# A decoder trunk on one core: a 64-byte smaller filler in front of the feed-forward's tiles, and the first weight load cut in two

## The chip, the core and the metric

The kernel runs on one core of a Trainium2 chip. The core has a matrix engine (TensorE; PE in the profile, with the loads of its stationary operand shown apart as PEld), VectorE (DVE), ScalarE (ACT), GpSimd (POOL) and SyncE (SP), and 16 DMA engines that move data between device memory and the on-chip memory SBUF. SBUF has 128 partitions; an address below is a byte offset within a partition. The metric is device time in microseconds of one execution; lower is better.

## The reference

Two layers, 256 tokens of width 1024, float32. Each layer is a sandwich: half a SwiGLU feed-forward, a token mixer, half a SwiGLU feed-forward. Layer 0 mixes with a sparse attention (compressed blocks, selected blocks, window), layer 1 with a sliding window with sinks. A final norm follows.

```python
def swiglu(x, w_gu, w_down):
    g, u = jnp.split(x @ w_gu, 2, axis=-1)
    return (jax.nn.silu(g) * u) @ w_down
...
for i in range(DEPTH):          # DEPTH = 2, D_MODEL = 1024, D_FF = 2816, SEQ = 256
    x = x + 0.5 * swiglu(rmsnorm(x, ffn1_norm[i]), ffn1_w_gu[i], ffn1_w_down[i])
    h = rmsnorm(x, mix_norm[i])
    y = nsa_mixer(h, ...) if kind == 0 else swa_mixer(h, ...)
    x = x + y
    x = x + 0.5 * swiglu(rmsnorm(x, ffn2_norm[i]), ffn2_w_gu[i], ffn2_w_down[i])
return rmsnorm(x, final_norm)
```

There are so four feed-forwards, called ffn 0 to ffn 3 here, in the order ffn 0, sparse attention, ffn 1, ffn 2, window attention, ffn 3.

## The kernel before, in words

**Precision.** Every float32 operand of a product is split into a rounded part `hi` (type float32r) and a rest `lo = value - hi`, and a product is the sum of three: hi by hi, hi by lo, lo by hi. Weights are split on the way: a piece of 1024 columns is loaded (`raw`, 5 buffers), ACT writes `hi`, DVE or POOL writes `lo` (4 buffers each). In the profile these are the lines L169 (load), L153 or L155 (`hi`), L183 (`lo`).

**A feed-forward.** The first half makes, for each of 22 blocks of 128 hidden units, the gate and the up part (`gu`). There the weights are the stationary operand (128 by 128) and the normalized, transposed input `xh` is the moving one: for each of 8 parts of the width, one matmul of 512 columns (`hi` of the weight by `hi` and `lo` of the input side by side) and one of 256 columns (`lo` of the weight by `hi` of the input), for gate and up each, in turn 512, 256, 512, 256. The result leaves through ACT and DVE, is gated, and is split into `hh` and `hl` (128 by 256 each), which stay in SBUF: 22 tiles of each, in the feed-forward's own pool. The second half (`dn`) turns the roles round: for each of the 22 blocks and each of the two halves of the tokens, a 128 by 128 part of `hh` or `hl` is the stationary operand and the split weight (`dn_h`, `dn_l`) moves, 512 columns wide: 22 x 2 x 3 = 132 matmuls for a block of 512 output columns, 264 in all. In ffn 3 the output columns are cut 512, 256, 256 (`LASTW`), so it has 132 matmuls of 512 columns and 264 of 256.

**Where tiles lie.** Pools take SBUF one after the other in the order in which they are opened: `const`, `weights`, `acts`, `small`, and then, one at a time in the same room, those of the feed-forwards, the two attentions, and `last`, which is opened before ffn 3 and stays in front of it. A tile called `fill_...` is never read or written; it only moves what comes behind it. Offsets inside tiles do the same on purpose: the `hi` part of the feed-forward's first weights starts 192 bytes into its tile (`PLACE_GU`), the inputs of the two attentions 64 bytes into theirs (`PLACE_NORM`), and ffn 3 has 448 bytes of filler of its own (`PLACE_H`). The table gives the places in the built program, as a remainder by 256.

| operand | stationary in | start, remainder by 256 |
|---|---|---|
| `gu_h` (hi of gate and up weights) | `gu` | 192 |
| `gu_l` (lo of the same) | `gu` | 0 |
| `hh`, `hl` of ffn 0, 1, 2 | `dn` | 64 |
| `hh`, `hl` of ffn 3 | `dn` | 0 |
| `xh` of the attentions | projections in (`nin`, `sin`) | 64 |
| `qs`, `vv` of the attentions | scores, weighted sums | 64 |
| `dn_h`, `dn_l`, `xh` of the feed-forwards | moving | 0 |

**The start.** The first norm and the first gate and up block are written by hand in order (`Norm.first`). TensorE multiplies zeros, then turns the first half of x, then takes the parts of the width as their weights come, in the order of `FIRST_K`. The first 2048 columns of weights come as four loads of 512. The first piece is split by two engines: POOL makes `hi` and `lo` of its columns 0 to 255, ACT and DVE those of 256 to 511 (L317). SP issues loads in order; the tile layer counts the completion of loads on eight counters in turn, and a load waits until the load eight before it has landed.

Of the kernel before, what the change touches and what calls it, by code (L numbers as in the profile page):

```python
# [91 lines left out]
def trunk_kernel(tc, x_in, wgu, wdn, nsa_in, nsa_w1, nsa_out, swa_in, swa_out, small, fgain, consts, out):  # L92
    nc = tc.nc
    from contextlib import ExitStack, contextmanager

    with ExitStack() as es:
# [3 lines left out]
        sp = es.enter_context(tc.tile_pool(name="small", bufs=1))  # L100
        pp = es.enter_context(tc.tile_pool(name="psum", bufs=1, space=PSUM))

        def fill(pool, name, n):

            pool.tile([P, n // 4], F32, name=f"fill_{name}")
# [7 lines left out]
        nc.gpsimd.memset(mhalf, -0.5)  # L113
        warm = cp.tile([P, NT], F32, name="warm")
        fill(cp, "const", 672)
        fill(sp, "small", 320)

        def mm(o, w, m, start, stop):
            nc.tensor.matmul(o, w, m, start=start, stop=stop)  # L119
# [7 lines left out]
        def s_bank(name):  # L127
            return pp.tile([P, 512], F32, tag="sc", bufs=BANKS["sc"], name=name)
# [31 lines left out]
        class Weights:  # L160
# [3 lines left out]
                self.src, self.name, self.kind, self.parts = src, name, name.rstrip("0123"), {}  # L164
                self.place = place

            def fetch(self, o, w, queue=nc.sync):
                raw = wp.tile([P, PIECE], F32, tag="raw", bufs=BUFS["raw"], name=f"{self.name}_r{o}")
                self.last = queue.dma_start(raw[:, :w], self.src[:, o:o + w]).ins  # L169
                return raw  # L170

            def split(self, o, raw, w, engines=None, starts=(0,)):
# [30 lines left out]
        def transposed(kp, norm, th, tl, tb, engine=None):  # L203

            ps = s_bank(f"xt{norm}_{kp}")
            for kk in range(2):
                for t in range(NT):
                    c = ((2 * kp + kk) % 4) * P
                    nc.tensor.transpose(ps[:, kk * S + t * P:kk * S + (t + 1) * P], x[t][kp // 2][:, c:c + P], ident)  # L209
            both = split_tile(f"xh{norm}_{kp}", PLACE_NORM[norm])  # L210
            hi, lo = both[:, :, 0, :], both[:, :, 1, :]

            def evict(kk):
                k = 2 * kp + kk
                g = prm[:, D_GAIN + norm * KD + k:D_GAIN + norm * KD + k + 1]
                if (engine or pick("xh")) == "A":
                    nc.scalar.activation(hi[:, kk, :], ps[:, kk * S:(kk + 1) * S], AF.Copy, scale=g)
                else:
                    nc.vector.tensor_scalar(hi[:, kk, :], ps[:, kk * S:(kk + 1) * S], g, None, ALU.mult)
                nc.vector.scalar_tensor_tensor(lo[:, kk, :], ps[:, kk * S:(kk + 1) * S], g, hi[:, kk, :],  # L220
                                               ALU.mult, ALU.subtract)
                th[k], tl[k], tb[k] = hi[:, kk, :], lo[:, kk, :], both[:, kk, :, :].rearrange("p a t -> p (a t)")

            return evict
# [4 lines left out]
        def squares(c0, c1, engine="A"):  # L229

            ss = sp.tile([P, NT], F32, tag="ss", bufs=3, name="ss")
            for t in range(NT):
                xc = columns(t, c0, c1)
                junk = ap_.tile([P, 512], F32, tag="junk", bufs=1, name="junk")
                if engine == "V":
                    nc.vector.tensor_tensor_reduce(out=junk[:, :c1 - c0], in0=xc, in1=xc, scale=1.0, scalar=0.0,
                                                   op0=ALU.mult, op1=ALU.add, accum_out=ss[:, t:t + 1])
                else:
                    nc.scalar.activation(junk[:, :c1 - c0], xc, AF.Square, accum_out=ss[:, t:t + 1])
            return ss  # L240

        def mean(j, v, ss):

            if j == 0:
                nc.vector.tensor_scalar(v, ss, 1.0 / D, EPS, ALU.mult, ALU.add)
            else:
                nc.vector.scalar_tensor_tensor(v, ss, 1.0 / D, v, ALU.mult, ALU.add)

        def row_scale(v, name):

            y = sp.tile([P, NT], F32, tag="rs_y", bufs=2, name=f"{name}_y")
            w = sp.tile([P, NT], F32, tag="rs_w", bufs=2, name=f"{name}_w")
            r = sp.tile([P, NT], F32, tag="rs_r", bufs=2, name=f"{name}_r")
            nc.gpsimd.tensor_tensor(y, v, mhalf, ALU.pow)
            nc.vector.tensor_mul(w, y, y)
            nc.vector.scalar_tensor_tensor(w, w, -0.5, v, ALU.mult, ALU.mult)
            nc.vector.scalar_tensor_tensor(r, w, 1.5, y, ALU.add, ALU.mult)
            return r

        class Norm:  # L260
# [18 lines left out]
            def first(self, wts, product, turn_scales):  # L279


                def load_x(t, h, queue):
                    queue.dma_start(x[t][h], x_in[t * P:(t + 1) * P, h * 512:(h + 1) * 512])

                evict = {}

                def turn(*kps):
                    for kp in kps:
                        evict[kp] = transposed(kp, 0, self.h, self.l, self.both, "A")

                def leave(*ks):
                    for k in ks:
                        evict[k // 2](k % 2)

                zeros = ap_.tile([P, 512], BF16, name="zeros")
                nc.vector.memset(zeros, 0.0)
                ps = s_bank("idle")

                def multiply_zeros(n):
                    for _ in range(n):  # L300
                        mm(ps, zeros[:, :P], zeros, True, True)

                multiply_zeros(8)
                load_x(0, 0, nc.sync)
                load_x(1, 0, nc.scalar)
                nc.sync.dma_start(ident, consts[:, C_ID:C_ID + P])
                nc.scalar.dma_start(prm[:, :D_SINK], small[:, :D_SINK])
                raw = [wts.fetch(o, 512) for o in (0, 512)]
                load_x(1, 1, nc.scalar)
                load_x(0, 1, nc.sync)  # L310
                raw += [wts.fetch(o, 512) for o in (1024, 1536)]
                nc.scalar.activation(warm, mhalf, AF.Exp)
                left = squares(0, 512, "V")
                turn(0, 1)
                multiply_zeros(3)
                leave(0, 2)
                wts.split(0, raw[0], 512, ("GG", "AV"), (0, 256))  # L317
                leave(1, 3)
                product(0, 0, 2)
                wts.split(512, raw[1], 512, "AV")  # L320
                turn(2, 3)
                product(0, 1, 3)
                leave(4, 6)
                wts.split(1024, raw[2], 512, "AV")
                leave(5, 7)
                wts.split(1536, raw[3], 512, "AG")
                product(0, 4, 5, 6, 7)
                wts.load(CHUNK, CHUNK, engines="VV")
                right = squares(512, 1024)
                mean(0, self.v, left)  # L330
                mean(1, self.v, right)
                self.r = row_scale(self.v, "n0")
                product(1, *range(KD))
                turn_scales()
# [225 lines left out]
        def weigh(pr, v_of, acc, pool, first, last, name):  # L560

            n_kt = pr.shape[2] // P
            for kt in range(n_kt):
                ps = s_bank(f"{name}_t{kt}")
                for hh in range(4):
                    nc.tensor.transpose(ps[:, hh * P:(hh + 1) * P], pr[:, hh, kt * P:(kt + 1) * P], ident)
                ph = pool.tile([P, 512], F32R, tag="ph", bufs=BUFS["ph"], name=f"{name}_h{kt}")
                pl = pool.tile([P, 512], F32R, tag="pl", bufs=BUFS["pl"], name=f"{name}_l{kt}")
                copy("ph", ph, ps)
                nc.vector.tensor_sub(pl, ps, ph)  # L570
                mm(acc, v_of(kt), ph, first and kt == 0, False)
                mm(acc, v_of(kt), pl, False, last and kt == n_kt - 1)
# [24 lines left out]
        def nsa(norm, nxt):  # L597
            with tc.tile_pool(name="nsa", bufs=1) as mp:
# [213 lines left out]
                def compressed(g, t, acc, first):  # L812
                    nm = f"cm{g}{t}"
                    ce = coarse.pop((g, t))
                    ps = s_bank(f"{nm}_c")
                    for hh in range(4):
                        nc.tensor.transpose(ps[:2 * NCP, hh * P:(hh + 1) * P],
                                            ce[:, hh, :, :].rearrange("p a n -> p (a n)").bitcast(F32), ident)
                    ph = mp.tile([P, 512], F32R, tag="ph", bufs=BUFS["ph"], name=f"{nm}_ch")
                    copy("pc", ph[:2 * NCP], ps[:2 * NCP])  # L820
                    mm(acc, vcs[:2 * NCP, g, :], ph[:2 * NCP], first, True)
# [228 lines left out]
```

## Time and profile before

| | |
|---|---|
| median of 3 runs | 1007.56 us (1004.36 to 1009.14) |
| the profiled execution | 1001.6 us |
| its span, first to last instruction | 999.8 us |
| mean granted TensorE clock | 0.996 of full |
| PE / PEld / DVE / ACT / POOL busy | 97 / 84 / 69 / 56 / 40 % of the span |
| read from device memory | 167.02 MB, 168 GB/s over the span |

PE busy means that some matmul was in flight; matmuls overlap, so how fast they follow each other is read from their starts, not from the busy share. The profiled execution was shorter than the three runs, so differences are taken within it.

### The profile page before, as it was taken

To read this page: it belongs to the slowest core of one execution; us is meant where nothing else is said; L and a number is where in the kernel's file an instruction comes from. 1 tells how busy PE (TensorE), PEld (TensorE's weight loads), DVE (VectorE), ACT (ScalarE), POOL (GpSimd) and SP (SyncE) were. 2 spreads that over 40 slices of the span, in tenths; PEclk is the share of its full clock that TensorE was granted. 3 is DMA by queue.
4 is the path that set the end of the run, shared out by engine and by line. 5 is a ranking of instruction groups with operands and counts; after the bars stand their busy time and mean duration, and the time that the engine had idled before them with its cause. 6 is when DMAs were issued, how large, how long until landed. Compare 5 with 4: busy or idle time off the path is not lost. (4 is left out here: it accounts for less than half of the span.)

```text
span 999.8 us, 15557 instructions
## 1 busy us (share of the span) xinstructions
PE 968.4 (97%) x5626; PEld 836.0 (84%) x5626; DVE 694.2 (69%) x1299; ACT 558.5 (56%) x1042; POOL 401.9 (40%) x400
## 2 busy tenths in 40 slices
PE   8999999998899999999999999999998899999997
PEld 6888888887787788888888888888897688888896
DVE  6887743467898888787435877864279988778533
ACT  6555544356767755555444555544358755655442
POOL 2534353465534225334431334363662013433443
PEclk9999999999999999999999999999999999999999
DMA  8676665543422256665666666656652266666651
GB/s 272 214 217 195 197 189 173 176 148 90 133 74 85 65 184 198 192 196 179 200 183 186 191 191 193 199 172 197 185 151 83 61 204 198 193 195 196 189 178 43
DMA packets 47741, 169.08 MB, mean 169 GB/s; under 512 B 5424, under 2 KB 5680, under 8 KB 47664
## 3 DMA queue, kind: packets, MB, share of 16 engines
q1 hardware_dynamic: 46800, 166.49, 54.8%
q10 hardware_dynamic: 864, 1.60, 0.4%
q8 instruction: 44, 0.72, 0.3%
q14 instruction: 33, 0.27, 0.1%
HBM read 167.02 MB, written 1.05 MB: 168 GB/s over the span
## 5 line engine op out<-in xcount | busy, mean ns | idle before, releaser
L119 PE MATMUL gu<-xh,gu_h 128*128 128x512 f32 x1408 | 479.8, 390 | 1.5 <-POOL gu_h L155 1.5
L119 PE MATMUL gu<-xh,gu_l 128*128 128x256 f32 x1408 | 388.1, 277 | 0.3 <-POOL gu_l L183 0.3
L119 PEld LDWEIGHTS gu<-xh,gu_h 128*128 128x128 f32 x1408 | 263.6, 188 | 55.7 <-POOL gu_h L155 2.0
L119 PEld LDWEIGHTS gu<-xh,gu_l 128*128 128x128 f32 x1408 | 264.1, 188 | 2.3 <-POOL gu_l L183 1.2
L183 DVE TENSOR_TENSOR gu_l<-gu_r,gu_h 128x1024 fp32r<-128x1024 f32 (+1 forms) x177 | 229.1, 1295 | 52.4 <-ACT gu_h L153 51.7
L153 ACT CAST gu_h<-gu_r 128x1024 fp32r<-128x1024 f32 (+2 forms) x178 | 184.6, 1039 | 71.4 <-PE gu L119 53.9
L153 ACT CAST dn_h<-dn_r 128x1024 fp32r<-128x1024 f32 (+1 forms) x89 | 92.5, 1041 | 114.5 <-PE dn L119 104.7
L119 PE MATMUL dn<-dn_l,hh 128*128 128x512 f32 (+1 forms) x396 | 146.7, 370 | 0.0
L119 PE MATMUL dn<-dn_h,hl 128*128 128x512 f32 (+1 forms) x396 | 146.6, 370 | 0.0
L119 PE MATMUL dn<-dn_h,hh 128*128 128x512 f32 (+1 forms) x396 | 146.4, 370 | 0.0
L183 DVE TENSOR_TENSOR dn_l<-dn_r,dn_h 128x1024 fp32r<-128x1024 f32 (+1 forms) x56 | 72.2, 1291 | 105.4 <-ACT dn_h L153 105.3
L158 POOL TENSOR_TENSOR hl<-u,hh 128x256 fp32r<-128x256 f32 x66 | 96.8, 1467 | 103.0 <-DVE hh L155 51.0
L183 POOL TENSOR_TENSOR dn_l<-dn_r,dn_h 128x512 fp32r<-128x512 f32 x66 | 86.8, 1336 | 110.3 <-ACT dn_h L153 109.2
L158 POOL TENSOR_TENSOR ga<-g,rb 128x256 f32<-128x256 f32 x88 | 74.6, 848 | 84.2 <-DVE g L464 79.7
L153 ACT COPY g<-gu 128x256 f32<-128x256 f32 x88 | 32.8, 372 | 109.9 <-PE gu L119 109.8
L119 PEld LDWEIGHTS dn<-dn_h,hh 128*128 128x128 f32 x396 | 74.8, 189 | 13.7
L119 PEld LDWEIGHTS dn<-dn_l,hh 128*128 128x128 f32 x396 | 74.8, 189 | 13.4
L119 PEld LDWEIGHTS dn<-dn_h,hl 128*128 128x128 f32 x396 | 74.8, 189 | 13.4
L119 PE MATMUL nin<-nin_h,xh 128*128 128x256 f32 (+1 forms) x320 | 62.0, 287 | 2.0 <-DVE r_b L489 1.7
L155 POOL CAST hh<-u 128x256 fp32r<-128x256 f32 x44 | 21.5, 488 | 94.1 <-DVE u L158 94.1
L464 DVE TENSOR_TENSOR g<-gu,g 128x256 f32<-128x256 f32 x88 | 37.2, 422 | 29.4 <-ACT g L153 29.0
L442 ACT ACTIVATE th<-ga 128x256 f32<-128x256 f32 x88 | 36.9, 419 | 33.6 <-POOL ga L158 27.6
(243 smaller groups left out, 1361.6 us busy)
## 6 DMA issues: line engine op xcount, KB each, us to landing
gu_r<-in_wgu_dram SPq DMA_DIRECT2D x174, 512.0 KB, 4.4
dn_r<-in_wdn_dram SPq DMA_DIRECT2D x87, 512.0 KB, 4.1
nin_r<-in_nsa_in_dram SPq DMA_DIRECT2D x18, 512.0 KB, 3.6
sin_r<-in_swa_in_dram SPq DMA_DIRECT2D x10, 512.0 KB, 3.5
nout_r<-in_nsa_out_dram SPq DMA_DIRECT2D x8, 512.0 KB, 3.6
sout_r<-in_swa_out_dram SPq DMA_DIRECT2D x8, 512.0 KB, 3.7
cmp_r<-in_nsa_w_dram SPq DMA_DIRECT2D x4, 512.0 KB, 4.4
gu_r<-in_wgu_dram SPq DMA_DIRECT2D x4, 256.0 KB, 5.7
```

What stands on the lines that cost most here:

```text
L119: nc.tensor.matmul(o, w, m, start=start, stop=stop)
L153: nc.scalar.copy(o, i)
L155: (nc.vector if c == "V" else nc.gpsimd).tensor_copy(o, i)
L158: (nc.vector if pick(key) == "V" else nc.gpsimd).tensor_tensor(o, a, b, op)
L183: eng.tensor_tensor(lo[:, q:e], raw[:, q:e], hi[:, q:e], ALU.subtract)
L442: nc.scalar.activation(th, ga, AF.Tanh, scale=0.5)
L464: nc.vector.tensor_tensor(g0, acc[0][:, :S], g0, ALU.add)
```

## The change

The filler in front of the pool `small` is 256 bytes long instead of 320. Everything that lies behind it, the small tiles and all tiles of the feed-forwards and attentions, moves down by 64 bytes; constants, x, weights, inputs `xh` and the attentions' outputs stay. `hh` and `hl` of ffn 0, 1 and 2 then start at remainder 0 by 256, those of ffn 3 at 192, and the attentions' `qs`, `kk` and `vv` at 0.

The first load of 512 columns of weights becomes two loads of 256 columns into the same tile; `fetch` takes a list of widths for that, and is always issued by SP.

```diff
-        fill(sp, "small", 320)
+        fill(sp, "small", 256)
...
-            def fetch(self, o, w, queue=nc.sync):
+            def fetch(self, o, *ws):
+
                 raw = wp.tile([P, PIECE], F32, tag="raw", bufs=BUFS["raw"], name=f"{self.name}_r{o}")
-                self.last = queue.dma_start(raw[:, :w], self.src[:, o:o + w]).ins
+                c = 0
+                for w in ws:
+                    self.last = nc.sync.dma_start(raw[:, c:c + w], self.src[:, o + c:o + c + w]).ins
+                    c += w
                 return raw
...
-                raw = [wts.fetch(o, 512) for o in (0, 512)]
+                raw = [wts.fetch(0, 256, 256), wts.fetch(512, 512)]
```

No instruction of PE, ACT, DVE or POOL is added, removed or moved. On SP one load is added at the start, and from there on the eight completion counters (`DMAHW0` to `DMAHW7`) are one place further for every load. Before, SP's first loads and what they wait for; `x_71` and `x_72` are the two halves of the first 128 tokens, `gu_r` the weights:

```order
L283 DMA x_71<-in_x_dram 128x512
L306 DMA ident<-in_consts_dram 128x128
L169 DMA gu_r_110<-in_wgu_dram 128x512
L169 DMA gu_r_112<-in_wgu_dram 128x512
L283 DMA x_72<-in_x_dram 128x512
L169 DMA gu_r_116<-in_wgu_dram 128x512 [waits DMAHW0_49]
L169 DMA gu_r_118<-in_wgu_dram 128x512 [waits DMAHW1_49]
L169 DMA gu_r_219<-in_wgu_dram 128x1024 [waits DMAHW2_49]
```

And now:

```order
L287 DMA x_71<-in_x_dram 128x512
L310 DMA ident<-in_consts_dram 128x128
L172 DMA gu_r_110<-in_wgu_dram 128x256 x2
L172 DMA gu_r_113<-in_wgu_dram 128x512
L287 DMA x_72<-in_x_dram 128x512 [waits DMAHW0_49]
L172 DMA gu_r_117<-in_wgu_dram 128x512 [waits DMAHW1_49]
L172 DMA gu_r_119<-in_wgu_dram 128x512 [waits DMAHW2_49]
L172 DMA gu_r_220<-in_wgu_dram 128x1024 [waits DMAHW3_49]
```

The wait for the first load, which stood before the third weight load, now stands before `x_72`. On ACT the same place of the program, the split of the first weights between the evictions of the turned x (`xh`), before:

```order
L217 ACTIVATE xh_0_131<-xt_0_126,prm 128x256 [waits DMAHW2_49,PE_49]
L217 ACTIVATE xh_1_137<-xt_1_132,prm 128x256 [waits PE_49]
L153 CAST gu_h_145<-gu_r_110 128x256 [waits DMAHW5_49]
L217 ACTIVATE xh_0_131<-xt_0_126,prm 128x256 [waits DVE_49]
L217 ACTIVATE xh_1_137<-xt_1_132,prm 128x256 [waits DVE_49]
L153 CAST gu_h_163<-gu_r_112 128x512 [waits DMAHW6_49]
```

And now:

```order
L221 ACTIVATE xh_0_132<-xt_0_127,prm 128x256 [waits DMAHW2_49,PE_49]
L221 ACTIVATE xh_1_138<-xt_1_133,prm 128x256 [waits PE_49]
L153 CAST gu_h_146<-gu_r_110 128x256 [waits DMAHW6_49]
L221 ACTIVATE xh_0_132<-xt_0_127,prm 128x256 [waits DVE_49]
L221 ACTIVATE xh_1_138<-xt_1_133,prm 128x256 [waits DVE_49]
L153 CAST gu_h_164<-gu_r_113 128x512 [waits DMAHW7_49]
```

ACT's half of the first weights now waits for a load of its own (counter 6), while POOL's cast of the other half (not shown) still waits for counter 5, on which now only the first 256 columns count.

## Rows read from the trace of the kernel before

**Rows 1.** The page, part 1: busy time and share of each engine.

```profile
PE 968.4 (97%) x5626; PEld 836.0 (84%) x5626; DVE 694.2 (69%) x1299; ACT 558.5 (56%) x1042; POOL 401.9 (40%) x400
```

**Rows 2.** Windows by stage: length, busy by engine (PE first), PEclk, DMA share, GB/s.

```profile
0.00:8.10 8.10, 5.40 (x20) 2.25 (x20) 2.65 (x8) 2.89 (x6) 0.70 (x6) 1.00 0.75 246
...
130.60:193.00 62.40, 62.40 (x274) 50.27 (x273) 22.75 (x28) 26.00 (x32) 25.17 (x20) 1.00 0.60 181
193.00:356.70 163.70, 149.46 (x1012) 129.61 (x1012) 133.87 (x378) 110.49 (x279) 75.28 (x73) 0.99 0.35 107
...
723.60:809.60 86.00, 79.23 (x530) 68.29 (x528) 72.22 (x185) 60.00 (x151) 25.52 (x37) 1.00 0.40 121
809.60:930.60 121.00, 121.00 (x715) 107.07 (x714) 96.84 (x154) 69.77 (x118) 44.74 (x48) 1.00 0.64 191
930.60:992.10 61.50, 61.50 (x397) 56.33 (x396) 26.55 (x31) 23.38 (x32) 28.64 (x24) 1.00 0.42 130
```

**Rows 3.** Groups on PE, 662 to 722 us: shapes, count | busy, mean ns | idle.

```profile
L119 PE MATMUL dn<-dn_h,hh 128*128 128x512 f32 x85 | 33.6, 396 | 0.0
```

**Rows 4.** Groups on PE, 931 to 960 us.

```profile
L119 PE MATMUL dn<-dn_h,hh 128*128 128x512 f32 x44 | 17.1, 389 | 0.0
```

**Rows 5.** Timeline of PE (start, us), first and last of 32 matmuls.

```profile
149.70 0.39 PE L119 MATMUL dn<-dn_l,hh 128*128 128x512 f32 x1
...
156.93 0.40 PE L119 MATMUL dn<-dn_h,hl 128*128 128x512 f32 x1
```

**Rows 6.** The same in ffn 3, first and last of 33 matmuls.

```profile
939.74 0.39 PE L119 MATMUL dn<-dn_l,hh 128*128 128x512 f32 x1
...
946.99 0.39 PE L119 MATMUL dn<-dn_h,hh 128*128 128x512 f32 x1
```

**Rows 7.** The same, ffn 3's narrow blocks, first and last of 60 matmuls.

```profile
969.83 0.28 PE L119 MATMUL dn<-dn_h,hl 128*128 128x256 f32 x1
...
976.90 0.28 PE L119 MATMUL dn<-dn_l,hh 128*128 128x256 f32 x1
```

**Rows 8.** The same, ffn 3's first half, first and last of 43 matmuls.

```profile
849.73 0.39 PE L119 MATMUL gu<-xh,gu_h 128*128 128x512 f32 x1
...
856.87 0.39 PE L119 MATMUL gu<-xh,gu_h 128*128 128x512 f32 x1
```

**Rows 9.** Chain that ended last: start, length, what.

```profile
726.79 9.32 PE sin L119 x80
```

**Rows 10.** Timeline at the start, all engines.

```profile
7.64 0.40 POOL L155 CAST gu_h<-gu_r 128x256 fp32r<-128x256 f32 x1 [6.81 <-DMA gu_r<-in_wgu_dram]
...
8.09 0.73 PE L119 MATMUL gu<-xh,gu_h 128*128 128x512 f32 x2 [1.51 <-POOL gu_h L155]
8.12 0.95 POOL L183 TENSOR_TENSOR gu_l<-gu_r,gu_h 128x256 fp32r<-128x256 f32 x1
```

**Rows 11.** Timeline at the start: SP's issues, and PE's second turn of x.

```profile
1.64 0.90 SPq L169 DMA_DIRECT2D gu_r<-in_wgu_dram  x2
...
2.59 0.43 SPq L283 DMA_DIRECT2D x<-in_x_dram  x1
...
4.30 13.11 SPq L169 DMA_DIRECT2D gu_r<-in_wgu_dram  x9
...
10.06 0.90 PEld L209 LDWEIGHTS xt<-ident,x 128*128 128x128 f32 x8
```

**Rows 12.** Groups on DVE, 541 to 661 us (ffn 2).

```profile
L464 DVE TENSOR_TENSOR g<-gu,g 128x256 f32<-128x256 f32 x21 | 8.9, 423 | 6.8 <-ACT g L153 6.7
```

**Rows 13.** Groups on DVE, 810 to 930 us (ffn 3).

```profile
L464 DVE TENSOR_TENSOR g<-gu,g 128x256 f32<-128x256 f32 x21 | 8.9, 423 | 7.3 <-ACT g L153 7.2
```

**Rows 14.** Waits of PE, 193 to 356.7 us: total, times, longest.

```profile
PE r_q L504 <- POOL r_sq L158: 3.2, 2, 2.1
PE hid L119 <- DVE na_mx L546: 1.9, 1, 1.9
```

**Rows 15.** Windows around a fall of the clock.

```profile
237.00:240.50 3.50, 3.50 (x19) 3.50 (x19) 3.02 (x13) 3.00 (x13) 0.53 (x1) 0.51 0.54 150
```

## The prediction

> **What bounds the kernel now.** I read the page's busy shares first: TensorE has work in flight for 97% of the span [rows 1]. Then the windows by stage [rows 2]: in the second halves of the feed-forwards (130.6 to 193.0 us, 930.6 to 992.1 us) and in the first halves (809.6 to 930.6 us) it is busy for the whole of its window, while no other engine is busy more than four fifths of it and the loads take 0.42 to 0.64 of the DMA engines. So there the time is the number of matmuls times the distance from one start to the next; what shortens that distance shortens the kernel. In the two attentions PE is free for 163.70 - 149.46 = 14.2 us and 86.00 - 79.23 = 6.8 us; there it waits for others. Before 8.1 us it waits for data.
>
> A busy PE hides what matters, so next I read starts. In the second half of ffn 0, 32 matmuls of 512 columns start between 149.70 and 156.93 us: 7.23 / 31 = 233.2 ns each [rows 5]. In the first block of ffn 3, same shape, same moving weights, same split work beside it, 33 start between 939.74 and 946.99: 7.25 / 32 = 226.6 ns [rows 6]. The groups say the same in another way: mean 396 ns in ffn 2, 389 ns in ffn 3 [rows 3, 4]. What is different in the program is where the stationary operands `hh` and `hl` lie: remainder 64 by 256 in ffn 0 to 2, remainder 0 in ffn 3. Neither stretch has a wait. I take it that the load of the next stationary operand, which runs beside the present matmul, disturbs the moving stream by an amount that depends on how the two addresses stand to each other.
>
> **The 64 bytes, ffn 0 to 2.** `hh` and `hl` move to remainder 0, the place of ffn 3 now; the moving weights stay. 3 x 264 = 792 matmuls by 233.2 - 226.6 = 6.6 ns are 5.2 us; by the group means (7 ns) 5.5 us. I take 5.4 us. All of it is on the path: PE is busy throughout, and the split work that feeds it (26.0 us ACT, 22.8 us DVE, 25.2 us POOL in 62.4 us [rows 2]) already keeps up at 226.6 ns in ffn 3. Late next would be the loads, at 181 GB/s now and 186 GB/s then, which the first halves exceed (191).
>
> [...]
>
> **The 64 bytes, ffn 3.** Its `hh` and `hl` leave remainder 0 for 192. For its 264 matmuls of 256 columns, 119.8 ns now (7.07 us / 59 [rows 7]), the nearest row is the first half: there a 256-column matmul runs beside the load of `gu_h`, at 192. A pair takes 7.14 us / 21 = 340.0 ns [rows 8]; less 226.6 for the 512-column one beside `gu_l`, at 0, leaves 113.4. The other row is the window attention's projection, 256 columns beside operands at 64: 9.32 us / 80 = 116.5 ns [rows 9]. I take 113.4: 264 x 6.4 ns = 1.7 us gained. The steps seen are about 6.6 ns; one step the wrong way (126.4) would lose 1.7 us. For its 132 matmuls of 512 columns no undisturbed row has 192; bounds are a step either way, 0.9 us gained or lost. I take 0, as 226.6 lies between.
>
> **The 64 bytes, attentions.** `qs`, `kk`, `vv` and the scores move from 64 to 0; the projections' `xh` and both outputs stay. The matmuls in question are, counted in the program, some 250 of 1542 in the two stages [rows 2], and moving and stationary operands move together, so their distance stays. I take 0, between 0.7 us gained (100 wide ones by a step) and 1.7 us lost (all by a step). For the elementwise engines the address does nothing that rows show: the same DVE operation takes 423 ns in ffn 2 and in ffn 3, whose tiles lie 64 bytes apart by remainder [rows 12, 13].
>
> **The load in two.** PE's first useful matmul waits 1.51 us, to 8.09, for POOL's cast, which starts at 7.64 when the first 512 columns have landed [rows 10]. After the change POOL needs 256 of them. The load was issued at 1.64 [rows 11] and took 6.0 us; x and the identity stand ahead of it in the queue. In the second or so before landing the queues move 246 GB/s or more [rows 2], so the 128 KB that POOL no longer waits for are about 0.5 us, more if x in ACT's queue takes its turn between them. I take 0.4 us earlier, between 0 and 0.75. The whole chain behind it (POOL's `lo`, 0.95 us, the second product, the turns of x at 10.06) follows PE, so it passes on. Against it: SP issues one load more, 0.45 us (0.90 for two [rows 11]), before the second weight load; this is covered, since data of the earlier loads still flow until about 7.6. The wait for the first load now holds `x_72`, which was issued at 2.59 and will go at about 4.3, when the third weight load went before; behind it in the queue stand the third and fourth weight loads and the next 1024-column pieces, each 0.4 us later. `x_72` is wanted at 10.06, 5.8 us after 4.3. If that cover were gone, PE would lose up to the 0.45 us of one issue. Later loads wait for a counter eight loads back, which five buffers have emptied long before: nothing.
>
> [...]
>
> **Sum.** 5.4 + 1.7 + 0 + 0 + 0.4 = 7.5 us. The profiled execution took 1001.6 us (span 999.8), so it would take 994.1. The three runs have a median of 1007.56, 6 us above it; the same difference gives 1007.56 - 7.5 = 1000.1 us, which I predict.
>
> **Rivals.** (a) The place is not the cause: what sets ffn 3's first block apart is something else, for instance that no further stage's weights are fetched behind it. Then only the start moves: 1007.56 - 0.4 = 1007.2. For it: it is one stage against three. Against it: DMA, ACT, DVE and POOL work at equal shares in both, and the `gu` rows show short distances too, with yet other places. [...] (b) ffn 0 to 2 gain, but 192 is a bad place for ffn 3's own stream: both widths lose a step, 264 x 6.6 + 132 x 6.6 ns = 2.6 us, and the start gives nothing: 1007.56 - 5.4 + 2.6 = 1004.8. For it: only a mixed stream has been seen at 192. Against: 113.4 is the shortest distance for 256 columns anywhere. (c) Slower: the attentions. PE waits 21.0 us there in all, for single late results (3.2 us for POOL's `r_sq`, 1.9 us for a DVE minimum [rows 14]) on engines that get in each other's way by chance of timing; all their operands move, and what starts them comes at another moment. If these waits grow by more than 7.5 us, a third, the change loses; at half as much again (10.5 us) it would be 1007.56 - 7.5 + 10.5 = 1010.6. Each stretch at the half clock adds to it: the granted clock was 0.51 from 237.0 to 240.5 [rows 15] just after PE had stood for that DVE result, which cost about half of 3.5 us. Against it: no instruction changes its order, and rows 12 and 13 show no effect of place on DVE. (d) That the two loads do not do what they should (POOL still waiting for both halves): the order shows separate counters, and it costs only 0.4 us: 1000.5, within the forecast.
>
> **How the numbers follow.** Forecast 0.71, (a) 0.09, (b) 0.12, (c) 0.05, (d) 0.03. The forecast's own terms lie between 5.2 - 1.7 - 0.9 - 1.7 = 0.9 and 5.5 + 1.7 + 0.9 + 0.7 + 0.75 = 9.6 us gained, but the ends need all at once; the runs of before spread by 2.4 us either way. Its own range is 997 to 1003.5; to hold 8 in 10, the whole reaches to (b): 996.0 to 1004.9. A measurement tells 0.5%, 5.0 us, from no change, so faster means below 1002.5. The forecast gives that with (d) in 0.65 of their 0.74 and (b) in 0.05: faster 0.70. Slower (above 1012.6) has 0.05, from (c) and from a bad set of runs; within 0.5% are 0.25.
>
> **What would show it.** In the changed kernel's profile: matmuls of 512 columns in the second halves of ffn 0 to 2 at a mean of 389 instead of 396 ns and each of these stages 1.8 us shorter (60.6 instead of 62.4); the 256-column ones of ffn 3 at 277 instead of 283 ns, its 512-column ones unchanged at 389; first halves unchanged; POOL's first cast at about 7.2 instead of 7.64 us, and PE's first product 0.4 us earlier. The prediction is wrong if the second halves keep 396 ns, if ffn 3's means rise, or if the attentions' windows (163.7 and 86.0 us) change by more than 1.5 us.

## The result and the profile after

The changed kernel took 997.49 us in the median of 6 runs (995.89 to 1001.42), the kernel before 1007.15 (6 runs, 1004.36 to 1009.14): a ratio of 0.991, with a 95% interval of 0.9885 to 0.9935. Faster by 9.1 us (6.5 to 11.6); 1000.1 us was predicted. Measured once more on another chip (e6 below), the ratio was 0.9938 (0.9918 to 0.9958), faster by 6.2 us. Both intervals hold the predicted gain of 7.5 us.

The profiled execution took 995.89 us, with a span of 994.1 instead of 999.8. The busy shares say as little as before [rows 1]:

```profile
PE 963.1 (97%) x5626; PEld 835.3 (84%) x5626; DVE 695.0 (70%) x1299; ACT 558.4 (56%) x1042; POOL 406.2 (41%) x400
```

The windows by stage, cut where the changed kernel's stages begin and end, in the order and with the columns of [rows 2]:

```profile
0.00:6.60 6.60, 4.95 (x19) 2.16 (x19) 2.31 (x7) 2.42 (x5) 0.70 (x6) 1.00 0.71 226
128.90:189.70 60.80, 60.80 (x274) 50.35 (x273) 22.78 (x28) 26.14 (x32) 25.07 (x20) 1.00 0.63 185
189.70:355.30 165.60, 150.74 (x1013) 130.97 (x1012) 134.80 (x378) 110.44 (x279) 76.06 (x73) 0.98 0.35 106
719.00:805.20 86.20, 79.48 (x530) 68.58 (x528) 72.40 (x185) 59.97 (x151) 25.56 (x37) 1.00 0.40 121
805.20:926.20 121.00, 121.00 (x715) 106.84 (x714) 96.90 (x154) 69.74 (x118) 44.75 (x48) 1.00 0.65 192
926.20:986.20 60.00, 60.00 (x397) 54.58 (x396) 27.30 (x30) 23.30 (x31) 28.72 (x24) 1.00 0.44 133
```

The second half of ffn 0 is down from 62.4 to 60.8 us, that of ffn 3 from 61.5 to 60.0, with the same matmuls (274 and 397 records) at the same granted clock, 1.00; the first half of ffn 3 keeps its 121.0. The sparse attention has become 1.9 us longer (163.7 to 165.6), at a mean clock of 0.98 instead of 0.99.

Read from the starts of the first and last matmul of each stage, the 5.7 us between the two spans are, after minus before: -1.65 by the end of ffn 0's first half, -4.91 in the second halves of ffn 0 to 2 (-1.68, -1.57, -1.66), -1.48 in that of ffn 3, 0.0 in the other first halves, +1.91 in the sparse attention, +0.24 in the window attention, +0.2 behind ffn 3.

The groups on PE, in ffn 2's second half (660 to 721 us) and in ffn 3's narrow blocks (956 to 984 us); the last two numbers of each are the busy time and the mean of one in ns:

```profile
L119 PE MATMUL dn<-dn_h,hh 128*128 128x512 f32 x85 | 33.1, 389 | 0.0
```

```profile
L119 PE MATMUL dn<-dn_h,hh 128*128 128x256 f32 x82 | 22.6, 276 | 0.0
```

The 512-column group has the mean that stood only in ffn 3 before, 389 instead of 396 ns [rows 3, 4]. The start, on all engines, and SP's first issues:

```profile
1.65 1.37 SPq L172 DMA_DIRECT2D gu_r<-in_wgu_dram  x3
...
4.48 0.33 SPq L287 DMA_DIRECT2D x<-in_x_dram  x1
...
6.17 0.40 POOL L155 CAST gu_h<-gu_r 128x256 fp32r<-128x256 f32 x1 [5.34 <-DMA gu_r<-in_wgu_dram]
6.57 0.41 ACT L153 CAST gu_h<-gu_r 128x256 fp32r<-128x256 f32 x1 [0.20 <-DMA gu_r<-in_wgu_dram]
...
6.62 0.74 PE L119 MATMUL gu<-xh,gu_h 128*128 128x512 f32 x2
```

POOL's cast starts at 6.17 and ACT's, which waits for the other half, at 6.57, each behind its own load; before, the two started together, 0.03 us apart. PE's first product stands at 6.62 instead of 8.09 [rows 10], and the second half of x is issued at 4.48 instead of 2.59 [rows 11].

### The profile page after: what moved, and what is told of

Same layout as the page of the kernel before. It is cut to its first block, busy times and chain, and to the rows that moved or that the text cites. A ratio compares the mean times of both kernels' runs of the same rounds, so it can differ in the third digit from the quotient of the medians.

```text
span 994.1 us, 15557 instructions
## 1 busy us (share of the span) xinstructions
PE 963.1 (97%) x5626; PEld 835.3 (84%) x5626; DVE 695.0 (70%) x1299; ACT 558.4 (56%) x1042; POOL 406.2 (41%) x400
## 5 line engine op out<-in xcount | busy, mean ns | idle before, releaser
L119 PE MATMUL dn<-dn_l,hh 128*128 128x512 f32 (+1 forms) x396 | 144.6, 365 | 0.0
L119 PE MATMUL dn<-dn_h,hl 128*128 128x512 f32 (+1 forms) x396 | 144.6, 365 | 0.0
L119 PE MATMUL dn<-dn_h,hh 128*128 128x512 f32 (+1 forms) x396 | 144.2, 364 | 0.0
L158 POOL TENSOR_TENSOR ga<-g,rb 128x256 f32<-128x256 f32 x88 | 77.4, 880 | 83.6 <-DVE g L468 79.1
```

What stands on the lines that cost most here:

```text
L158: (nc.vector if pick(key) == "V" else nc.gpsimd).tensor_tensor(o, a, b, op)
```

## The experiments

Differences of median times are ratios with their 95% intervals; what a mechanism does is read from the length of a stage and from the distance from one start to the next, since the second halves of one kernel repeat to 0.1 us (before and e5, changed and e6), while its times lie up to 5.5 us apart (995.89 to 1001.42, 1004.36 to 1009.14). "Remainder" is the start address by 256, "distance" the remainder of the stationary operand less that of the moving one.

**e1: the 64 bytes alone.** The kernel before with

```diff
-        fill(sp, "small", 320)
+        fill(sp, "small", 256)
```

> The filler of 256 bytes alone; the first weights stay one load. Theory of the place: the three wide second halves lose 1.65 us each and ffn 3's 1.5 us, 6.4 us in all, so about 1000.7 us against 1007.2, ratio 0.9937; the start stays at 8.1 us. Rival, that most of the gain is the start's (the timed kernels differ by 9.7 us, the stages of the profiles by 6.4): the same 6.4 us here, and the missing 3 us with the split load alone. Rival, that the place does nothing: 1007 us and a mean of 396 ns for the wide matmuls.

Measured: 1000.66 us (9 runs) against 1006.07 (23 runs), ratio 0.9952 (0.9936 to 0.9968). The second halves took 60.77, 60.91, 60.81 and 60.02 us, as in the changed kernel. In windows (40 to 120 us, a part of ffn 0's first half; ffn 0's second half; sparse attention; window attention):

```profile
40.00:120.00 80.00, 80.00 (x459) 70.05 (x458) 61.85 (x93) 44.62 (x76) 30.14 (x34) 1.00 0.67 198
134.10:194.80 60.70, 60.70 (x274) 50.31 (x273) 22.59 (x28) 26.13 (x32) 25.11 (x20) 1.00 0.63 185
194.80:361.30 166.50, 152.44 (x1013) 132.52 (x1013) 134.10 (x378) 110.86 (x279) 75.38 (x73) 0.97 0.35 105
725.00:811.00 86.00, 79.32 (x529) 68.39 (x528) 72.28 (x185) 60.15 (x151) 25.66 (x37) 1.00 0.40 121
```

The whole gain of the second halves belongs to the 64 bytes. By the stages that is 6.4 us; the time of the whole kernel gives 4.8 us (3.2 to 6.4), so the stages stand at the upper end of what the time allows.

**e2: the two loads alone.** The changed kernel with the old filler:

```diff
-        fill(sp, "small", 256)
+        fill(sp, "small", 320)
```

> The load in two alone, with the filler at 320 bytes. My forecast was 0.4 us earlier, 1006.8 us. The profiles show PE's first product at 6.6 instead of 8.1 us: then 1.5 us, 1005.7 us, ratio 0.9985. Rival, that the start is worth what the stages don't explain of the timed difference: 3 us, 1004.2 us, ratio 0.997. Second halves at 396 ns in every case.

Measured: 1005.85 us (12 runs), ratio 0.9995 (0.9981 to 1.001). The second halves are the old ones, 62.48, 62.50, 62.48 and 61.50 us:

```profile
132.10:194.60 62.50, 62.50 (x275) 50.17 (x274) 22.72 (x28) 26.07 (x32) 25.24 (x20) 1.00 0.62 181
194.60:361.10 166.50, 152.52 (x1013) 132.54 (x1012) 134.10 (x378) 110.86 (x279) 75.28 (x73) 0.97 0.34 105
```

PE's first product stood at 7.13 us. By the clock on the whole kernel the two loads are worth between 1.9 us gained and 1.0 lost; the time cannot tell more.

**e3: stay, and move the other operand.** The kernel before, in which the split weights of all second halves begin 64 bytes into their tiles, so that both operands lie at 64 in ffn 0 to 2:

```diff
-                rows_product(Weights(wdn[i], f"dn{i}"), NF, hh, hl, residual(quarter, nxt), f"dn{i}")
+                rows_product(Weights(wdn[i], f"dn{i}", (64, 64)), NF, hh, hl, residual(quarter, nxt), f"dn{i}")
```

> The kernel before with the moving weights of the second halves (hi and lo) also 64 bytes further into their tiles. If the distance between stationary and moving operand decides (0 in ffn 0 to 2, 192 in ffn 3), it does for the second halves what the change does: 389 ns in ffn 0 to 2, 277 ns for ffn 3's narrow ones, about 1000.7 us. If the place of the stationary operand alone decides, 396 and 283 ns stay and the time is 1007 us.

Measured: 1001.07 us (6 runs), ratio 0.9943 (0.9923 to 0.9964); second halves 60.81, 60.89, 60.79 and 60.02 us. The group on PE in 660 to 721 us, a stretch that lies mostly in ffn 2's second half in either kernel, for e3 and then for e2:

```profile
L119 PE MATMUL dn<-dn_h,hh 128*128 128x512 f32 x84 | 32.7, 389 | 0.0
```

```profile
L119 PE MATMUL dn<-dn_h,hh 128*128 128x512 f32 x78 | 30.8, 395 | 0.0
```

With `hh` and `hl` still at 64, the stream is as quick as with both operands at 0. So in these stages the distance of the two operands counts (60.8 us at 64 and 64 as at 0 and 0, 62.5 at 64 and 0), not the place of either.

**e4: ffn 3 back at remainder 0.** The changed kernel with 64 bytes more in ffn 3's own filler:

```diff
-PLACE_H = (0, 0, 0, 448)
+PLACE_H = (0, 0, 0, 512)
```

> The changed kernel with ffn 3's own filler at 512 instead of 448 bytes, so that its stationary operands lie at remainder 0 again. Theory of the place: ffn 3's second half goes back from 60.0 to 61.5 us (narrow matmuls 283 ns, wide ones 389 ns in all three kinds), the rest stays: 999.0 us, 1.5 above the changed kernel. If the gain in ffn 3 came from elsewhere, it keeps 60.0 us.

Measured: 1000.75 us (5 runs) against 1006.07, ratio 0.9947 (0.9926 to 0.9967). ffn 0 to 2 keep their 60.81, 60.92 and 60.81 us, ffn 3's second half is back at 61.50, and its 256-column matmuls are back at 283 ns, 120 ns from start to start:

```profile
L119 PE MATMUL dn<-dn_h,hh 128*128 128x256 f32 x68 | 19.2, 283 | 0.0
```

So 192 is worth 1.48 us to ffn 3, as a sum of two signs. Its 264 narrow matmuls went from 119.9 to 113.3 ns (-1.75 us); its 132 wide ones from 226.9 to 228.9 ns (+0.26 us), in a turn of 226, 229 and 232 for the three kinds of product. The turn does not belong to the kinds: in e9 to e11, further down, the same three distances stand with other kinds (229, 232 and 226 in e9).

**e5, e6: the two kernels again, on another chip.** No edit.

> The kernel before, one look more. If ffn 0's first half has two speeds by chance, not by kernel, it may show 125.5 us here in place of 122.5 with blocks 2 to 21 at 350 ns a pair; then the first profile of before was a lucky one, 3 us below a usual one. If the speed belongs to the kernel, 122.5 us again. Second halves 62.5, 62.5, 62.5, 61.5 us either way.

> The changed kernel once more. First measured at 997.5 against 1007.2 us (9.7 less), while its two parts alone gave 5.4 and 0.2 us less, and the kernel with ffn 3 back at 0 (1.5 us more by its stage) 5.3 us less. Theory that the parts add up: 6 to 7 us less, ratio 0.993 to 0.994, and the profile shows ffn 0's first half at either 122.4 us (340 ns a pair from block 2 on, as in the first two profiles) or 125.5 us (350 ns, as in the four others), by chance. Rival, that both parts together do more than each alone: 9 to 10 us less again, ratio 0.990, with ffn 0's first half at 122.4 us.

Measured: e5 1005.38 us (one execution); e6 999.17 us (6 runs, 994.72 to 1001.54) against 1005.2 (11 runs), the second ratio given above. That is the sum of the parts (0.993 to 0.994) and not the 0.990 of the rival. Windows of e5, then of e6, over the stretches shown for e1:

```profile
40.00:120.00 80.00, 80.00 (x459) 70.00 (x458) 61.79 (x95) 44.96 (x75) 31.04 (x33) 1.00 0.67 198
131.90:194.40 62.50, 62.50 (x275) 50.19 (x274) 22.73 (x28) 26.00 (x32) 25.26 (x20) 1.00 0.62 180
194.40:360.50 166.10, 152.09 (x1012) 132.34 (x1011) 133.95 (x378) 110.49 (x279) 75.16 (x73) 0.97 0.34 105
727.50:813.40 85.90, 79.14 (x529) 68.26 (x528) 72.19 (x185) 60.03 (x151) 25.52 (x37) 1.00 0.40 121
```

```profile
40.00:120.00 80.00, 80.00 (x472) 70.76 (x472) 62.56 (x99) 45.10 (x79) 44.99 (x36) 1.00 0.69 206
129.40:190.20 60.80, 60.80 (x274) 50.32 (x274) 22.76 (x28) 26.07 (x32) 25.15 (x20) 1.00 0.63 185
190.20:354.10 163.90, 149.54 (x1012) 129.80 (x1011) 133.76 (x378) 110.49 (x279) 75.30 (x73) 0.99 0.35 107
717.80:804.10 86.30, 79.59 (x530) 68.66 (x529) 72.50 (x185) 59.97 (x151) 25.62 (x37) 1.00 0.40 121
```

The second halves repeat to 0.1 us in both. The sparse attention does not: the kernel before now needs 166.1 us and the changed one 163.9, the other way round from the first two profiles. Its length goes with its granted clock, which was 0.99, 0.98 or 0.97 in the rows above. In the changed kernel's first profile there are two falls of the granted clock, to 0.50 of full speed:

```profile
242.90:246.30 3.40, 3.40 (x15) 3.30 (x16) 1.55 (x2) 0.50 (x2) 1.00 (x1) 0.50 0.75 222
256.50:259.90 3.40, 3.20 (x15) 2.85 (x15) 1.62 (x3) 1.42 (x4) 2.63 (x3) 0.50 0.47 135
```

Before had one such stretch [rows 15], e6 one, e5, e1 and e2 three each: 163.65 and 163.98 us with one, 165.56 with two, 166.18, 166.46 and 166.5 with three, so 1.3 us for each. The other seven profiles bear it out: 163.75 and 164.62 us with one (e11, e7), 165.34 to 165.87 with two (e8 to e10), 166.06 and 166.27 with three (e3, e4). What sets how many there are, no run shows. At equal numbers of them the shift costs the sparse attention 0.3 us at most (e5 to e1; before to e6), and e2, without the shift, is as long as e1.

**e7, e8: the other two distances.** The changed kernel with a filler of 384 or 192 bytes, which puts `hh` and `hl` of ffn 0 to 2 at 128 or 192, and those of ffn 3 at 64 or 128:

```diff
-        fill(sp, "small", 256)
+        fill(sp, "small", 384)      # e7;  192 in e8
```

> The changed kernel with the filler at 384 bytes: stationary operands of ffn 0 to 2 at remainder 128, of ffn 3 at 64. Theory of the distance: ffn 3's wide matmuls at 233 ns from start to start (as ffn 0 to 2 before), its narrow ones near the 116.5 ns of the attention's projection; for ffn 0 to 2 at 128 no row exists, between 226 and 240 ns. A step of about 6.6 ns per 64 bytes, 64 being the next best to 0, would give 240.

> The filler at 192 bytes: stationary operands of ffn 0 to 2 at 192, of ffn 3 at 128. Theory of the distance: the wide matmuls of ffn 0 to 2 as ffn 3's wide ones in the changed kernel (226, 229 and 232 ns for the three kinds), 229 in the mean, so a stage of 61.3 us, 0.5 us more than at 0; ffn 3's at 128 unknown, within 113 and 127 ns for the narrow ones.

Measured (one execution each): 1002.72 and 1003.68 us. The second halves took 62.22, 62.25, 62.24 and 60.61 us in e7, 61.33, 61.96, 61.33 and 61.88 in e8. The narrow blocks of ffn 3, in e7 (at 64) and e8 (at 128):

```profile
L119 PE MATMUL dn<-dn_h,hh 128*128 128x256 f32 x77 | 21.3, 276 | 0.0
```

```profile
L119 PE MATMUL dn<-dn_h,hh 128*128 128x256 f32 x74 | 20.8, 281 | 0.0
```

The expectations came true for the wide matmuls of ffn 3 in e7 (233) and for ffn 0 and 2 in e8 (61.3 us). Two missed: the narrow ones of ffn 3 at 64 took 113.3 ns and not 116.5, and ffn 1 in e8 took 61.96 us, since the second of its two blocks of output columns ran at 233.3 ns where the first, and both blocks of ffn 0 and 2, ran at 228.9.

From all profiles so far, ns from start to start inside the blocks of the second halves:

| distance by 256 | 0 | 64 | 128 | 192 |
|---|---|---|---|---|
| 512 columns | 226.7 | 233.3 | 232.3 to 232.4 | 228.9, once 233.3 |
| 256 columns | 120.0 | 113.3 | 118.7 | 113.3 |

The best distance for 512 columns, 0, is the worst for 256. For each feed-forward the change took the quickest of the four distances. At 0 and at 64 the wide matmuls never left their value: 226.7 ns in each of 28 second halves, 233.3 in each of 10, over all thirteen profiles (for ffn 3 its one wide block). At 192 one distance has shown two values, for the wide ones here and for the narrow ones in e9 to e11.

**e9, e10, e11: the first halves.** e5 and e1 had shown that ffn 0's first half can run at two paces: 472 matmuls in the 80 us above in e6, 459 in e5, e1. Three places of the gate and up weights were tried in the changed kernel, to see whether another one frees it of the slower pace:

```diff
-                wts = Weights(wgu[i], f"gu{i}", (PLACE_GU, 0))
+                wts = Weights(wgu[i], f"gu{i}", (64, 0))      # e9;  (192, 192) in e10, (64, 64) in e11
```

> The changed kernel with the hi part of the gate and up weights at remainder 64 by 256 instead of 192, lo left at 0. ffn 0's first half has shown two speeds, 340 ns (226 + 114) or 350 ns (232 + 118) for a pair of matmuls, in the same kernel; the first block and the others always have different ones, so one profile shows both. Theory A (the two speeds are two offsets of the stationary load against the moving stream, on top of the address distance): the 256-column matmuls, which run beside the load of hi, change, to 113 in one of the speeds or 119 to 121, and with them the pair in one of the speeds; ffn 1 to 3 stay at one speed, at 227 + 113 = 340 or 227 + 119 = 346. Theory B (the speeds have nothing to do with the address): 340 and 350 as before everywhere. If ffn 1 to 3 lose 6 ns a pair, 3 x 352 pairs cost 6 us.

> The changed kernel with hi and lo of the gate and up weights both at remainder 192 by 256 (before hi 192, lo 0). The 512-column matmuls run beside the load of lo. By the distances measured in the second halves (0: 227, 192: 229 ns) ffn 1 to 3 go from 340 to 342 ns a pair, 0.7 us for each. Theory A (two offsets on top of the distance): ffn 0's slow speed, 350 ns, changes by more than 2 ns a pair; if it falls to 345 or less, the changed kernel's slow executions gain over 1.5 us. Theory B: 350 stays 350 or becomes 352.

> The changed kernel with hi and lo of the gate and up weights both at remainder 64 by 256. By the distances of the second halves (512 columns at 64: 233.5 ns; 256 columns at 64: 113.3) ffn 1 to 3 go from 340 to 347 ns a pair, 2.4 us for each, 7 us in all. Theory A (two offsets on top of the distance): ffn 0's two speeds change their places or come together. Theory B: ffn 0 shows 347 and 357.

Measured (one execution each): 1011.09, 1014.47 and 1013.72 us, beside 1008.02 for the kernel before. ffn 1's first half took 124.50, 125.58 and 125.58 us where the changed kernel has 120.99. In windows of 80 us in it, the changed kernel first, then e9 and e10:

```profile
380.00:460.00 80.00, 80.00 (x473) 70.87 (x472) 62.95 (x97) 45.34 (x76) 33.23 (x34) 1.00 0.67 197
```

```profile
380.00:460.00 80.00, 80.00 (x459) 70.36 (x459) 61.27 (x96) 45.56 (x76) 31.02 (x33) 1.00 0.64 191
```

```profile
380.00:460.00 80.00, 80.00 (x455) 69.64 (x454) 60.74 (x94) 44.85 (x76) 31.00 (x32) 1.00 0.65 190
```

Neither theory holds over the three. No place kept 340 ns for a pair of 512 and 256 columns: 232 + 118 = 350 in e9, 233.5 + 119.8 = 353 in e10 (in a turn of three), 235 + 118 = 353 in e11, against the 340 to 347 that were expected from the table of distances. In e9 the wide matmul slowed by 5 ns, from 227 to 232, although the operand loaded beside it had not moved. So in this alternating stream the distance of one load to one stream is not enough; the place of the other load counts too, by a rule that these runs do not give. ffn 0 was never quicker than the others here (353 to 354 in all three), so the places tried only lose.

## Why the prediction was right, and where it was not

**ffn 0 to 2, 5.4 us.** Shown. Inside the blocks the distance went from 233.3 to 226.7 ns, just as read from rows 5 and 6, and 792 times that step is 5.3 us. The stages gained 4.91 us: the rest, about 0.4 us, is missing where a stage or its second block of columns begins, which the sum had left out. The 5.4 us leaned on the group means, which read 7 ns for a step of 6.67. e1 alone has the gain, e2 alone hasn't, and e7 and e8 set the stages to lengths of their own. The predicted signs came: 389 ns; 60.8 us where 60.6 was named.

The prediction laid the effect to how the two addresses stand to each other, and e3 shows that: the same gain (60.81, 60.89 and 60.79 us) with the stationary operand unmoved. The distance of the operands makes 227 or 233 ns of the same 512 columns. That it is the load of the next operand that disturbs the stream, as the prediction took it, is not shown; shown is that the two addresses count together.

**ffn 3, 1.7 us for the narrow matmuls and 0 for the wide.** Narrow 1.75 us (283 to 276 ns in the groups), shown by e4, which takes it back. The wide term was 0.26 us lost, within its bounds of 0.9 either way, but "its 512-column ones unchanged at 389" was wrong, and with it one of the signs set for a failure, "if ffn 3's means rise", came up for the wide ones (928 to 953 us of the changed kernel):

```profile
L119 PE MATMUL dn<-dn_h,hl 128*128 128x512 f32 x37 | 14.6, 394 | 0.0
L119 PE MATMUL dn<-dn_l,hh 128*128 128x512 f32 x37 | 14.5, 392 | 0.0
L119 PE MATMUL dn<-dn_h,hh 128*128 128x512 f32 x37 | 14.4, 388 | 0.0
```

For the narrow ones the prediction had set 116.5 ns beside the 113.4 it took, from the window attention [rows 9]. That was a misreading: 9.32 us runs from the first start to the last end and holds the first gap of 193 ns. From start to start that projection stands at 113 to 114 ns too.

**The attentions, 0, and rival (c).** Another sign set for a failure, a window changed by more than 1.5 us, did come up: the sparse attention took 1.9 us more in the first profile. It is not the shift: e6 has the changed kernel at 163.98 us and e5 the kernel before at 166.18, and the length follows the number of stretches at half clock, 1.3 us for each. The waits on which (c) rested are as before (PE for POOL's `r_sq` 3.5 us in two, for the DVE minimum 1.9 us, against 3.2 and 1.9 [rows 14]). The sign was badly chosen, since one profile of before could not show how much that stage varies by itself.

**The start, 0.4 us, and rival (d).** The mechanism is as told, POOL waits for its own half only (its cast at 6.17 us, ACT's at 6.57), so (d) falls. The size was too small: 0.4 us, between 0 and 0.75, against 1.1 in the mean of the profiles, and it swings from one execution to the next. PE's first product stood at 8.09, 6.96, 8.53 and 8.00 us without the split (before, e5, e1, e3) and at 6.62, 7.13, 6.35, 6.95, 6.83 and 6.66 with it (changed, e2, e4, e6, e7, e8; e9 to e11 have 6.58, 6.58 and 7.06): a mean of 7.90 for the four against 6.75 for the nine. The prediction had priced the 128 KB that POOL no longer waits for, about 0.5 us; POOL's first cast in fact starts 1.2 us earlier in the mean (6.02 against 7.25 us). Why it is more than the bytes stays open. Only four profiles are without the split, and one of them, e5, lies among those with it. In e2 POOL's cast started at 5.40 and the product 1.7 us later, after the last part of the turned x had been written at 6.98: there the weights came early, and the turned x was what came last. So the earliest start moved less (6.96 without the split in e5, 6.35 with it in e4) than the latest (8.53 in e1, 7.13 in e2). Where ACT's cast waited for its load of the other half, it began 0.40, 0.44, 0.80 and 1.02 us behind POOL's (changed, e7, e4, e10). The longest of these, in e10:

```profile
6.13 0.40 POOL L155 CAST gu_h<-gu_r 128x256 fp32r<-128x256 f32 x1 [5.30 <-DMA gu_r<-in_wgu_dram]
...
7.15 0.40 ACT L153 CAST gu_h<-gu_r 128x256 fp32r<-128x256 f32 x1 [0.80 <-DMA gu_r<-in_wgu_dram]
```

**Rivals (a) and (b).** (a), that place is not the cause, falls with e1 to e3. (b), that 192 is a bad place for ffn 3, falls with e4.

**The sum.** 4.91 + 1.48 us of second halves, about 1.1 at the start and 0.25 back in the window attention are 7.2 us, against 7.5 predicted and 9.1 (6.5 to 11.6) and 6.2 (4.2 to 8.2) measured. That the sum came so close is in part luck: the second halves gave 0.7 us less than the 7.1 named for them, the start 0.7 more. The same terms with other signs of chance make up each pair of profiles: 5.7 us between the first two profiles, 10.7 between e5 and e6, of which 2.55 are ffn 0's pace and 2.2 the half clock.

## What to carry to other kernels

Where TensorE is the bound, read the distance from start to start in undisturbed stretches and compare stages of the same shape: 6 ns in 230 are worth finding (4.91 us of the kernel here), and a filler that sets the distance of the stationary to the moving operand by 256 bytes may be all they need. The best distance must be measured for each width and each order of widths, since a table from one stream did not hold in another (347 ns a pair expected in e11, 353 measured), and at the distance 192 not even in one stream (228.9 and 233.3 ns in e8). Before a small difference between two profiles is put down to an edit, profile the same kernel twice and take the stages apart; here chance alone moved two stages by 2 to 3 us each.

## What was not expected of the hardware

**Two paces of one stream.** ffn 0's first half takes 122.4 us in three profiles (before, changed, e6) and 125.0 to 125.8 in seven (e1 to e5, e7, e8). From block 2 to its end every pair takes 340 ns in the one case, 226 + 114, and 350 in the other, 232 + 118; block 1, counted from 0, has the other pace in nine of the ten (in e6 it has the quick one like the rest). In a window of the kernel before in its first profile, to be set beside the one of e5 above:

```profile
40.00:120.00 80.00, 80.00 (x472) 70.77 (x471) 63.20 (x98) 45.54 (x77) 33.04 (x34) 1.00 0.67 204
```

472 matmuls against 459 in the same 80 us of the same program, at a granted clock of 1.00, with PE busy throughout. Between blocks 1 and 2 stand two matmuls of 128 columns (`rb`); in nine of ten profiles the pace changes there, and in all ten it then stays. What sets it, and why ffn 1 to 3 always keep the quicker pace with the weights at 192 and 0, was not found. It is worth about 3 us. That the profiled execution of before lay 6 us under the median of its runs fits this and the clock: it had the quick pace and one stretch at half clock. The timed executions point the same way: six of the changed kernel, over both measurements, have a mean granted clock of 0.995, and their spans are 994.1 us (the one of the first profile, at the quick pace) and 994.7 in two and 996.7 to 997.4 in four. That this gap is the pace of ffn 0 is likely and not shown.

**The window attention's first projection** also has two: 80 matmuls of 256 columns in 9.32 us before [rows 9], 9.31 in e5, 9.33 in e1 and e2, but 9.66 in the changed kernel and e6. From start to start that is 113 to 114 ns or 117 to 119:

```profile
722.15 9.66 PE sin L119 x80
```

e4, which differs from the changed kernel only behind this stage, took 9.34, and e3, which has the old filler, 9.66, so this too comes and goes; it is the +0.24 us of that attention.

**A pace may be handed on.** In e9 to e11, whose first halves ran at 350 ns and more, ffn 3's second half took 61.20 us instead of 60.02, though its code and places are the changed kernel's: its 256-column matmuls stood at 118 ns instead of 113, the same two values as in the window attention. In e9:

```profile
L119 PE MATMUL dn<-dn_h,hh 128*128 128x256 f32 x84 | 23.4, 279 | 0.0
```

In the four kernels with ffn 3 at the distance 192 behind a first half at 340 ns (changed, e1, e3, e6) it was 113 each time. That the stream before decides is the simplest reading of seven profiles; it was not tried by itself.
